# Layer A's first product group: the sums of squares and their factors taken one block later, two squares and a few constants traced later

## Chip, cores, metric

The kernel runs on one core of one Trainium2 chip. The metric is the time of one execution on the device in microseconds (us), as the median of several runs; lower is better. Of each kernel one execution is also recorded by the profiler.

## What is computed

A trunk of two layers on one sequence of 2048 tokens of 1024 values, in float32. The change is in the first projection of the first layer (A). Cut to what matters there:

```python
def rmsnorm(x, g):
    y = x * lax.rsqrt(jnp.mean(x * x, axis=-1, keepdims=True) + EPS)
    return y * g

# layer A
u = rmsnorm(h, norm_a_g[i])
proj = u @ w_in_a[i]                    # q, k, v, forget logits, gate
q, k, v, f_logit, gate = split(proj)
q = rmsnorm(q.reshape(b, s, 16, 64), qnorm_a_g[i])
k = rmsnorm(k.reshape(b, s, 16, 64), knorm_a_g[i])
...
o = fox_attention(q, k, v, log_f)       # causal, with a forget bias
h = h + (o * silu(gate)) @ w_out_a[i]
# shared k, v; layer B: sliding-window attention, gate, projection
```

## The kernel before, in words

**Products.** The 2048 tokens are 16 blocks of 128 (`tb`). A product in float32 is made of three products of rounded parts: the high part of the tokens with the high and the low part of the weights, and the low part of the tokens with the high part of the weights. One block times 512 columns of weights is 8 steps (`dt`, 128 rows of the weights each) of three matmuls, 24 matmuls at L757, all added up in one PSUM tile `b2`. There are three such tiles, so block n writes where block n-3 was read out. The products of layer A come in groups of columns; the first group (`gi == 0`) is half of the values `v`.

**The norm.** The gain is folded into the weights (`split_weight`, L484 high part on ScalarE, L485 low part on VectorE), and the row factor 1/sqrt(mean of squares) is applied when a block's products are read out. So the products need no factor, but the read-out does. In layer A the tokens come transposed from memory (`turned`). A block of them passes through: the load (L369, by SyncE's queue), the cast to the high part (L383, ScalarE), the low part (L384, VectorE), the square in place (L389, ScalarE), the sum over the 8 pieces (L391, VectorE, into a tile `ro2`, of which there are two), the sum over partitions (`block_sums`, L400, two small products with a column of ones for a pair of blocks, each recorded as two matmuls), and `rstd`, a chain of six small instructions (L357 VectorE, L358 square root on ScalarE, L359 to L363 VectorE), which writes the factors `r` of the pair.

**When.** `factor(tb, dt)` is called ahead of each step of the first group. At an even block's step 0 it issues the squares of that block and the next, at the same block's step `FACTOR_AT` = 7 the sums over partitions and the chain. After a block's 24 matmuls come its read-out: for the first group `v_tile`, L539 on ScalarE and L540 on VectorE into a tile `st`, then its store (L543). The blocks' loads and these tiles share four slots `st`; odd blocks up to the eleventh and the next group's weights (L438) share two slots `wr`. Loads run three blocks ahead (`LOADED_AHEAD`). At block 8 `vectors()` issues 13 small loads of gains on SyncE's queue, at block 11 `angles()` makes the sine and cosine tables, with one `Sin` on ScalarE at L327 that needs another function table than the square root.

**The order.** The framework's scheduler puts the instructions of each engine into a fixed queue when the kernel is built: among those whose inputs it estimates as ready and whose slots are free, the one that stands first in the program. Where `keep_in_program_order` is called (L400, the small loads), an instruction stays behind all that the program gave its engine earlier. On the chip each engine works its queue in order.

**Constants.** `constants()` makes `ident` on GpSimd, and from it on VectorE `fold` (L227, twice L229, L230) and `identb` (L232). Both are first used in the attention of layer A.

Of the kernel before, what the change touches and what calls it, by code (L numbers as in the profile page):

```python
# [17 lines left out]
ALU = mybir.AluOpType  # L18
# [4 lines left out]
P = 128  # L23
S = 2048
D = 1024
NTB = S // P
NDT = D // P
# [31 lines left out]
LOADED_AHEAD = 3  # L59
QK_LAG = 1  # L60

FACTOR_AT = 7
ROW_AT = 2

JOBS_AT = (0, 3, 6, 9)
# [84 lines left out]
class Trunk:  # L150
# [56 lines left out]
    def constants(self):  # L207
        nc, cp, a = self.nc, self.const, self.a

        def select(view, src, pattern, base, cm, fill):  # L210
            nc.gpsimd.affine_select(
                out=view, in_=src, pattern=pattern, compare_op=ALU.is_ge,
                fill=fill, base=base, channel_multiplier=cm,
            )

        def tile_(name, shape, dt=F32):
            return cp.tile(shape, dt, name=name, tag=name)

        self.ones = tile_("ones", [P, P])
        nc.gpsimd.memset(self.ones, 1.0)  # L220
        self.tri = tile_("tri", [P, P])
        select(self.tri, self.ones, [[1, P]], 0, -1, 0.0)
        self.ident = tile_("ident", [P, P])
        select(self.ident, self.tri, [[-1, P]], 0, 1, 0.0)

        self.fold = tile_("fold", [P, 32])
        nc.vector.tensor_tensor(self.fold, self.ident[:, :32], self.ident[:, 32:64], ALU.add)  # L227
        for c in (64, 96):
            nc.vector.tensor_tensor(self.fold, self.fold, self.ident[:, c : c + 32], ALU.add)  # L229
        nc.vector.tensor_single_scalar(self.fold, self.fold, 2.0, ALU.mult)  # L230
        self.identb = tile_("identb", [P, P], BF16)
        nc.vector.tensor_copy(self.identb, self.ident)  # L232

        self.mask_s = tile_("mask_s", [P, 2, P], BF16)
        nc.gpsimd.memset(self.mask_s, 0.0)
        for i in range(2):
            select(self.mask_s[:, i], self.mask_s[:, i], [[1, P]], 0, -1, NEG)

        self.band = tile_("band", [P, 2, P], BF16)
        nc.gpsimd.memset(self.band, 0.0)  # L240
        select(self.band[:, 0, :], self.band[:, 0, :], [[1, P]], -1, -1, NEG)
        select(self.band[:, 1, :], self.band[:, 1, :], [[-1, P]], 0, 1, NEG)

        self.loads = []
        warm = tile_("warm", [P, 1])
        nc.scalar.activation(warm, self.ones[:, :1], AF.Sqrt)

        def vector(name, n, views):
            t = tile_(name, [P, n])
            for rows, src in views:  # L250
                self.loads.append((t[rows], src))
            return t

        def column(name, src, n):
            return vector(name, n, [(slice(0, P), src.rearrange("(t p) -> p t", p=P))])

        def pair_column(name, src):
            col = src.rearrange("(p o) -> p o", o=1)
            return vector(name, 1, [(slice(0, HD), col), (slice(HD, P), col)])

        def row(name, src, n):
            return vector(name, n, [(slice(0, P), src.to_broadcast([P, n]))])

        self.g_a = column("g_a", a["norm_a_g"][0], NDT)
        self.bf = row("bf", a["b_forget"], H)
        self.g_qa = pair_column("g_qa", a["qnorm_a_g"][0])
        self.g_ka = pair_column("g_ka", a["knorm_a_g"][0])
        self.g_b = column("g_b", a["norm_b_g"][0], NDT)
        self.g_kv = column("g_kv", a["kv_norm_g"], NDT)
        self.g_qb = pair_column("g_qb", a["qnorm_b_g"][0])  # L270
        self.g_kb = pair_column("g_kb", a["knorm_b_g"])
        self.sink = row("sink", a["sinks"], H)
        self.gq16 = row("gq16", a["qnorm_b_g"][:, :ROT], ROT)
        self.nsink = tile_("nsink", [P, H])
# [6 lines left out]

    def vectors(self):

        nc = self.nc
        self.load_vectors(self.loads[1:])
        for t in (self.g_qb, self.g_kb):
            for s in range(2):
                nc.vector.memset(t[s * HD : s * HD + ROT, :], 1.0)
        nc.vector.tensor_single_scalar(self.nsink, self.sink, -1.0, ALU.mult)
# [274 lines left out]
    def normer(self, src):  # L564


        nc, turned = self.nc, len(src.shape) == 4
        uh, ul, blocks, small = {}, {}, {}, {}
        factors = self.sb("r", [P, NTB], bufs=1)
        done = [0, 0]  # L570

        def parts(tb):
            ch, t0 = divmod(tb * P, CH)
            if ch not in uh:
                uh[ch] = self.sb("big", [P, NDT, CH], F32R)
                ul[ch] = self.sb("big", [P, NDT, CH], F32R)
            return (u[ch][:, :, t0 : t0 + P] for u in (uh, ul))

        def load(tb):
            blocks[tb] = xt = self.load_block(src, tb)  # L580
            if not turned:
                _, junk = parts(tb)
                if tb % 2 == 0:
                    small[tb] = self.sb("sm", [P, 4, 8], bufs=4)
                ss = small[tb // 2 * 2][:, 0, tb % 2 : tb % 2 + 1]
                nc.scalar.activation(
                    junk, xt.rearrange("p (c t) -> p c t", t=P), AF.Square, accum_out=ss
                )

        def fetch(n, loads=()):  # L590
            while done[0] < min(n, NTB):
                load(done[0])
                done[0] += 1
                for other in loads:
                    other()
                loads = ()

        def upto(n, loads=()):

            while done[1] < min(n, NTB):  # L600
                fetch(done[1] + LOADED_AHEAD, loads)
                loads = ()
                tb = done[1]
                self.split_block(blocks[tb], turned, *parts(tb))
                done[1] += 1

        def factor(tb, dt):

            both = (tb, tb + 1)
            if tb % 2:  # L610
                return
            if turned and dt == 0:
                for b in both:
                    blocks[b] = self.block_squares(blocks[b])
            if dt == FACTOR_AT:
                sm = self.sb("sm", [P, 4, 8], bufs=4) if turned else small[tb]
                ss = self.block_sums([blocks[b] for b in both], tb) if turned else None
                self.rstd(sm, 2, D, ss=ss, out=factors[:, tb : tb + 2])

        return upto, factor, uh, ul, factors, fetch  # L620

    def projections(self, normed, groups, row, later=None, pre=None, hook=None, first=None):
# [75 lines left out]
        for gi, grp in enumerate(groups):  # L698
# [35 lines left out]
                continue  # L734
            q, v = grp.get("qk"), grp.get("v")
            rope = self.rotary(q["rope"]) if q and "rope" in q else None
            late = []
            for tb in range(NTB):
                norm(tb + NORM_AHEAD)
                if gi == 1 and tb == ROW_AT:  # L740
                    self.rstd_row(factors, row)
                r0 = factors[:, tb : tb + 1]
                if gi == 0 and pre is not None and tb in pre:
                    pre[tb]()
                if tb in FORGET_AT and forget:
                    forget.pop(0)()
                if gi and tb in JOBS_AT and jobs:
                    jobs.pop(0)()
                us = slice(tb % 4 * P, (tb % 4 + 1) * P)
                ps = self.ps("b2", [P, CH])  # L750
                for dt in range(NDT):
                    if hook is not None and gi == len(groups) - 1:
                        hook(tb, dt)
                    if gi == 0:
                        factor(tb, dt)
                    for i, (u, k) in enumerate(((uh, 0), (uh, 1), (ul, 0))):
                        nc.tensor.matmul(  # L757
                            ps[:, :n], u[tb // 4][:, dt, us], W[k][dt],
                            start=(dt == 0 and i == 0), stop=(dt == NDT - 1 and i == 2),
                        )  # L760
                if len(late) > QK_LAG:
                    late.pop(0)()
                if q is not None:
                    c0 = q["c0"]
                    qn = self.qk_norm(
# [9 lines left out]
                if v is not None:  # L775
                    self.v_tile(
                        ps[:, v["c0"] : v["c0"] + v["nh"] * HD], v["nh"],
                        v["dst"][v["h0"] : v["h0"] + v["nh"], tb * P : (tb + 1) * P, :].rearrange(
                            "h t e -> t h e"
                        ),  # L780
                        r0,
                    )
            for job in late:
                job()
            if grp.get("forget"):
# [784 lines left out]
```

## Time and profile before

| | us |
|---|---|
| median of 3 runs | 2504.49 |
| lowest and highest run | 2503.91, 2506.16 |
| profiled execution, its own time | 2501.05 |
| its span (first to last instruction) | 2499.3 |

In the span TensorE (PE) is busy 98%, VectorE (DVE) 72%, ScalarE (ACT) 52%, GpSimd (POOL) 37%. The rows that a page or a view gives are read like this: in a row of the timeline stand the start from the span's begin, the duration, the engine, the line of the kernel, the operation, what it writes and reads, the number of instructions merged into the row, and in brackets the idle time of the engine ahead of it with what ended it. SPq is SyncE's queue of DMA issues; PEld is TensorE's loading of the stationary operand, beside its matmuls. Buffer numbers are left out of names, so that `b` is a tile `b2`. The first group of products runs from about 8 to 105 us.

### The profile page before, as it was taken

What the parts mean: (1) busy time and instruction counts of PE and PEld (TensorE: products, weight loads), DVE (VectorE), ACT (ScalarE), POOL (GpSimd) and SP (SyncE); (2) the same over time, 40 slices, a digit from 0 to 9 for tenths busy, and PEclk for the clock granted to TensorE, in tenths of its full rate; (3) what the DMA queues carried; (4) which work ended last, traced back from release to release, by engine and by line L of the source; (5) the groups of instructions that cost most, each with busy time, mean ns of one, the idle gap of its engine ahead of it and who ended that gap; (6) DMA issues with size and microseconds to landing.
All of it is one profiled execution on the core that took longest, in us unless ns stands there. A gap on an engine that the chain in (4) does not pass through costs nothing.

```text
span 2499.3 us, 37273 instructions
## 1 busy us (share of the span) xinstructions
PE 2450.7 (98%) x12256; PEld 2048.9 (82%) x12256; DVE 1798.3 (72%) x4279; ACT 1307.5 (52%) x2553; POOL 920.6 (37%) x611
## 2 busy tenths in 40 slices
PE   8999999999999999999999999999999999899999
PEld 6788899988888887877877778888888888788887
DVE  7656667736888888888888965556666434888885
ACT  5423333414777777777777761145332213677674
POOL 0000000013777777777777752200011001355543
PEclk9999999999999999999999999999999999999999
DMA  5656545687545655565465559965443424665561
GB/s 183 201 160 190 174 147 157 192 273 220 147 144 157 192 147 157 145 198 150 131 193 166 153 168 291 287 214 165 114 127 88 128 97 143 188 170 159 160 170 64
DMA packets 351520, 419.29 MB, mean 168 GB/s; under 512 B 64928, under 2 KB 248256, under 8 KB 345152
## 3 DMA queue, kind: packets, MB, share of 16 engines
q1 hardware_dynamic: 351328, 416.92, 57.3%
q8 instruction: 97, 1.59, 0.3%
q14 instruction: 95, 0.78, 0.1%
HBM read 265.29 MB, written 151.40 MB: 167 GB/s over the span
## 4 chain that ended last, share of the span: by engine, by line
PE 48%; DVE 4%; DMA 2%; ACT 2%; issue 1%; POOL 1%; SPq 0%; POOLq 0%; ACTq 0%; DVEq 0%
PE b L757 9%; PE pb L1404 6%; PE b L1220 5%; PE pa L1025 4%; PE pb L1059 3%; PE pb L720 3%; PE b L720 3%; PE b L347 2%; PE mx L934 2%; PE sc L983 2%; PE pa L1337 2%; PE sc L982 2%; DMA wr<-wg 1%; PE b L1282 1%; PE b L1279 1%
## 5 line engine op out<-in xcount | busy, mean ns | idle before, releaser
L757 PE MATMUL b<-wh,big 128*128 128x512 f32 (+3 forms) x2560 | 769.9, 375 | 8.9 <-ACT wh L484 8.9
L1001 POOL TENSOR_TENSOR big<-st,big 128x1024 fp32r<-128x1024 f32 (+1 forms) x320 | 659.7, 2076 | 273.6 <-ACT big L1000 171.8
L757 PEld LDWEIGHTS b<-wh,big 128*128 128x128 f32 x2560 | 471.4, 188 | 79.3 <-ACT wh L484 10.9
L757 PE MATMUL b<-wl,big 128*128 128x512 f32 (+3 forms) x1280 | 473.7, 370 | 1.7 <-DVE wl L485 1.7
L1010 DVE TENSOR_TENSOR ac<-ac,st 128x512 f32<-128x512 f32 (+3 forms) x576 | 355.0, 616 | 53.2 <-ACT st L997 24.5
L997 ACT ACTIVATE st<-sc 128x512 f32<-128x512 f32 (+1 forms) x512 | 274.9, 584 | 157.6 <-PE sc L983 79.4
L1025 PE MATMUL pa<-big 128*128 128x512 f32 (+3 forms) x1280 | 327.1, 370 | 3.1 <-POOL big L1001 1.0
L1000 ACT CAST big<-st 128x1024 fp32r<-128x1024 f32 (+1 forms) x320 | 295.5, 924 | 8.0
L757 PEld LDWEIGHTS b<-wl,big 128*128 128x128 f32 x1280 | 241.4, 189 | 38.3 <-DVE wl L485 5.8
L1025 PEld LDWEIGHTS pa<-big 128*128 128x128 f32 x1280 | 222.8, 190 | 49.1 <-ACT sq L1033 16.8
L945 DVE CUSTOM_DVE_ANT_0 mx<-mx,rot 128x128 f32<-128x128 f32 (+3 forms) x240 | 210.5, 877 | 39.6 <-PE mx L934 34.5
L493 ACT ACTIVATE sq<-b,r 128x512 f32<-128x512 f32 (+2 forms) x128 | 77.8, 608 | 301.2 <-PE b L757 298.1
L982 PE MATMUL sc<-big 128*128 128x512 f32 (+3 forms) x640 | 231.1, 365 | 1.3 <-DVE st L540 1.1
L983 PE MATMUL sc<-big 67*128 67x512 f32 (+3 forms) x640 | 229.7, 368 | 0.0
L934 PE MATMUL mx<-big 66*128 66x128 f32 (+3 forms) x660 | 192.1, 365 | 10.4 <-DVE mt L945 9.8
L1059 PE MATMUL pb<-wh,wr 128*128 128x512 f32 x488 | 179.4, 399 | 3.7 <-DMA wr<-wg 3.1
L495 DVE TENSOR_REDUCE sm<-sq 128x8 f32<-128x512 f32 (+2 forms) x128 | 74.9, 585 | 138.9 <-ACT sq L493 138.7
L857 POOL MEMSET rot<- 128x1024 bf16 x1 | 1.0, 952 | 421.0 <-PE pb L347 421.0
L934 PEld LDWEIGHTS mx<-big 66*128 66x128 f32 x660 | 113.6, 191 | 50.0 <-DVE mt L945 20.2
L1307 POOL TENSOR_TENSOR st<-st,rs 128x1024 f32<-128x1024 f32 (+1 forms) x64 | 118.0, 1843 | 93.4 <-DVE rs L1306 88.1
L982 PEld LDWEIGHTS sc<-big 128*128 128x128 f32 x640 | 121.7, 190 | 23.2 <-DVE st L540 1.5
L983 PEld LDWEIGHTS sc<-big 67*128 67x128 f32 x640 | 121.7, 190 | 21.2
(258 smaller groups left out, 4349.3 us busy)
## 6 DMA issues: line engine op xcount, KB each, us to landing
wr<-wg SPq DMA_DIRECT2D x62, 512.0 KB
va<-st SPq DMA_DIRECT2D x32, 512.0 KB
ka<-st SPq DMA_DIRECT2D x64, 256.0 KB
ut<-big SPq DMA_DIRECT2D x16, 1024.0 KB
big<-ka SPq DMA_DIRECT2D x16, 1024.0 KB
big<-qa SPq DMA_DIRECT2D x16, 1024.0 KB
qb<-st SPq DMA_DIRECT2D x64, 256.0 KB
big<-qb SPq DMA_DIRECT2D x16, 1024.0 KB
```

What stands on the lines that cost most here:

```text
L720: nc.tensor.matmul(ps, W[k][dt][:, ft * P : (ft + 1) * P], u[ch][:, dt, :], start=(dt == 0 and i == 0), stop=(dt == NDT - 1 and i == 2),)
L757: nc.tensor.matmul(ps[:, :n], u[tb // 4][:, dt, us], W[k][dt], start=(dt == 0 and i == 0), stop=(dt == NDT - 1 and i == 2),)
L934: mm = nc.tensor.matmul(ps[:, b, :wb], qb[:66, i * P : (i + 1) * P], kb[:66, k0 + b * wb : k0 + (b + 1) * wb], start=True, stop=True,)
L945: nc.vector.tensor_tensor_reduce(out=lg, in0=lg, in1=mask, scale=1.0, scalar=NEG, op0=ALU.add, op1=ALU.max, accum_out=f_(o),)
L982: nc.tensor.matmul(o, ka[:, ks], qa[:, qs], start=not (last and n_), stop=False)
L983: nc.tensor.matmul(o, kb[:, ks], qb[:, qs], start=False, stop=not diag)
L997: nc.scalar.activation(pf[:, off : off + w], ps[:, :w], AF.Exp, scale=HD**-0.5)
L1000: nc.scalar.copy(ph[:, :tw], pf[:, :tw])
L1001: nc.gpsimd.tensor_tensor(pl[:, :tw], pf[:, :tw], f_(ph[:, :tw]), ALU.subtract)
L1010: nc.vector.tensor_tensor(a_, a_, pf[:, off : off + w], ALU.add)
L1025: nc.tensor.matmul(pv[:, q0 : q0 + w], v[:, k, :], src[:, off : off + w], start=(p == 0 and n_ == 0 and i == 0), stop=(last and n_ == 1 an ...
L1059: nc.tensor.matmul(ps, w[:, dt // 2 % 2, wk, dt % 2, :], us[dt][uk], start=(dt == 0 and i == 0), stop=(dt == NDT - 1 and i == 2),)
```

## The change

Four edits, all in the first group of layer A or ahead of it. (1) `factor`: the sums over partitions and the chain of a pair are issued at the odd block's step 3 (`TURNED_AT`) in place of the even block's step 7, four steps later. (2) The read-out of an even block, which needs the factor, is held until then: the read-out is now a function `evict`, and for an even block of layer A's first group it is issued at the next block's step 3, behind the chain; an odd block's stays behind its matmuls. (3) The squares of blocks 0 and 1 are issued at block 0's step 6 (`SQUARES_AT`) in place of step 0; those of the other pairs stay at the even block's step 0. (4) `fold` and `identb` are made in `vectors()`, at block 8, behind the issue of its small loads. Layer B's use of these functions keeps its order.

```diff
         self.fold = tile_("fold", [P, 32])
-        nc.vector.tensor_tensor(self.fold, self.ident[:, :32], self.ident[:, 32:64], ALU.add)
-        for c in (64, 96):
-            nc.vector.tensor_tensor(self.fold, self.fold, self.ident[:, c : c + 32], ALU.add)
-        nc.vector.tensor_single_scalar(self.fold, self.fold, 2.0, ALU.mult)
         self.identb = tile_("identb", [P, P], BF16)
-        nc.vector.tensor_copy(self.identb, self.ident)
...
     def vectors(self):
...
         self.load_vectors(self.loads[1:])
+        nc.vector.tensor_tensor(self.fold, self.ident[:, :32], self.ident[:, 32:64], ALU.add)
+        for c in (64, 96):
+            nc.vector.tensor_tensor(self.fold, self.fold, self.ident[:, c : c + 32], ALU.add)
+        nc.vector.tensor_single_scalar(self.fold, self.fold, 2.0, ALU.mult)
+        nc.vector.tensor_copy(self.identb, self.ident)
...
         def factor(tb, dt):
 
-            both = (tb, tb + 1)
-            if tb % 2:
-                return
-            if turned and dt == 0:
-                for b in both:
+            t0 = tb // 2 * 2
+            if turned and (tb, dt) == (t0, 0 if tb else SQUARES_AT):
+                for b in (t0, t0 + 1):
                     blocks[b] = self.block_squares(blocks[b])
-            if dt == FACTOR_AT:
+            if (tb, dt) == ((t0 + 1, TURNED_AT) if turned else (t0, FACTOR_AT)):
                 sm = self.sb("sm", [P, 4, 8], bufs=4) if turned else small[tb]
-                ss = self.block_sums([blocks[b] for b in both], tb) if turned else None
-                self.rstd(sm, 2, D, ss=ss, out=factors[:, tb : tb + 2])
+                ss = self.block_sums([blocks[b] for b in (t0, t0 + 1)], tb) if turned else None
+                self.rstd(sm, 2, D, ss=ss, out=factors[:, t0 : t0 + 2])
...
                     if gi == 0:
                         factor(tb, dt)
+                        if held and dt == TURNED_AT:
+                            held.pop()()
...
                 if len(late) > QK_LAG:
                     late.pop(0)()
+                if gi == 0 and pre is not None and tb % 2 == 0:
+                    held.append(partial(evict, ps, tb))
+                else:
+                    evict(ps, tb)
```

## Rows read from the trace of the kernel before

**Rows 1.** The page: the span, and the busy time, share of the span and instructions of each engine.

```profile
span 2499.3 us, 37273 instructions
...
PE 2450.7 (98%) x12256; PEld 2048.9 (82%) x12256; DVE 1798.3 (72%) x4279; ACT 1307.5 (52%) x2553; POOL 920.6 (37%) x611
```

**Rows 2.** Busy time of the engines in three stretches of the first group (start and end in us, length, then busy us and instructions of PE, PEld, DVE, ACT, POOL, the granted clock of TensorE, the share of the DMA engines, GB/s).

```profile
8.24:17.40 9.16, 8.30 (x27) 5.61 (x28) 9.02 (x16) 7.07 (x10) 0.00 (x0) 1.00 0.65 256
28.50:85.10 56.60, 56.60 (x258) 46.98 (x259) 39.78 (x59) 26.98 (x35) 0.00 (x0) 1.00 0.68 195
85.10:105.20 20.10, 18.56 (x84) 15.06 (x84) 16.74 (x41) 11.28 (x16) 0.00 (x0) 1.00 0.52 138
```

**Rows 3.** The waits of the first 130 us, those of TensorE and of its weight loads among them (who waited for whom, us in total, times, longest).

```profile
PE b L757 <- ACT wh L484: 8.9, 2, 8.2
...
PE pa L400 <- DVE ro L391: 1.8, 3, 0.8
PE b L757 <- DVE wl L485: 1.1, 2, 0.9
...
PEld b L757 <- DVE st L540: 0.4, 1, 0.4
```

**Rows 4.** The timeline of VectorE in the first 17 us: the weights' low parts (L485), block 0's sum of squares (L391) and the first three of the five constants' instructions (L227, L232, L229); the last two (L229, L230) lie ahead of the second and of the third L485 row.

```profile
8.22 1.42 DVE L485 SCALAR_TENSOR_TENSOR wl<-big,g_a,wh 128x512 fp32r<-128x512 f32 x2 [1.57 <-ACT wh L484]
9.78 1.98 DVE L391 TENSOR_REDUCE ro<-st 128x128 f32<-128x1024 f32 x1
11.67 0.18 DVE L227 TENSOR_TENSOR fold<-ident 128x32 f32<-128x32 f32 x1
11.77 0.22 DVE L232 CAST identb<-ident 128x128 bf16<-128x128 f32 x1
11.91 0.18 DVE L229 TENSOR_TENSOR fold<-fold,ident 128x32 f32<-128x32 f32 x1
12.01 0.74 DVE L485 SCALAR_TENSOR_TENSOR wl<-big,g_a,wh 128x512 fp32r<-128x512 f32 x1
...
12.77 0.75 DVE L485 SCALAR_TENSOR_TENSOR wl<-big,g_a,wh 128x512 fp32r<-128x512 f32 x1
...
13.52 2.73 DVE L485 SCALAR_TENSOR_TENSOR wl<-big,g_a,wh 128x512 fp32r<-128x512 f32 x4
```

**Rows 5.** The timeline of TensorE: its first matmul, and the sums over partitions (L400) of the pairs (2,3), (4,5), (6,7), (12,13) and (14,15), the last two in two parts, with the first matmul behind the sums of (4,5), and the pair of matmuls with which block 14 ends and block 15 begins.

```profile
8.24 0.79 PE L757 MATMUL b<-wh,big 128*128 128x512 f32 x1 [8.24 <-ACT wh L484]
...
28.22 0.50 PE L400 MATMUL pa<-ones,ro 128*128 128x1 f32 x4
...
39.61 0.50 PE L400 MATMUL pa<-ones,ro 128*128 128x1 f32 x4
39.97 0.49 PE L757 MATMUL b<-wh,big 128*128 128x512 f32 x1
...
50.99 0.50 PE L400 MATMUL pa<-ones,ro 128*128 128x1 f32 x4
...
85.16 0.28 PE L400 MATMUL pa<-ones,ro 128*128 128x1 f32 x2
86.20 0.38 PE L400 MATMUL pa<-ones,ro 128*128 128x1 f32 x2 [0.77 <-DVE ro L391]
...
97.45 0.28 PE L400 MATMUL pa<-ones,ro 128*128 128x1 f32 x2
98.50 0.38 PE L400 MATMUL pa<-ones,ro 128*128 128x1 f32 x2 [0.77 <-DVE ro L391]
...
99.29 0.83 PE L757 MATMUL b<-wh,big 128*128 128x512 f32 x2
```

**Rows 6.** The timeline of VectorE from 79 to 100 us: sums of squares of blocks 12 and 13 (L391), the first and the last step of the chain of the pair (10,11) (L357, L363), and the read-outs of blocks 10 and 11 and of 12 and 13 (L540).

```profile
79.83 2.02 DVE L391 TENSOR_REDUCE ro<-st 128x128 f32<-128x1024 f32 x1 [1.13 <-ACT st L389]
81.77 0.15 DVE L357 TENSOR_SCALAR sm<-pa 128x2 f32<-128x2 f32 x1
...
83.55 0.16 DVE L363 SCALAR_TENSOR_TENSOR r<-sm 128x2 f32<-128x2 f32 x1
84.18 1.97 DVE L391 TENSOR_REDUCE ro<-st 128x128 f32<-128x1024 f32 x1 [0.47 <-ACT st L389]
86.06 1.39 DVE L540 SCALAR_TENSOR_TENSOR st<-b,r,st 128x512 fp32r<-128x512 f32 x2
...
98.81 1.41 DVE L540 SCALAR_TENSOR_TENSOR st<-b,r,st 128x512 fp32r<-128x512 f32 x2 [0.37 <-ACT st L539]
```

**Rows 7.** The timeline of ScalarE: a weight of the second group (L484, at block 11's products), and from 94 us the square roots of the pairs (12,13) and (14,15) (L358), the table loads, `Sin` (L327) and the read-outs of blocks 12 and 13 (L539).

```profile
69.39 0.71 ACT L484 ACTIVATE wh<-wr,g_a 128x512 fp32r<-128x512 f32 x1
...
94.02 0.20 ACT L358 ACTIVATE sm<-sm 128x2 f32<-128x2 f32 x1
...
96.49 1.28 ACT L327 ACT_TABLE_LOAD   x1
97.78 0.42 ACT L327 ACTIVATE cossin<-cossin 128x256 f32<-128x256 f32 x1
98.11 1.25 ACT L539 ACTIVATE st<-b,r 128x512 fp32r<-128x512 f32 x2
99.37 1.28 ACT L358 ACT_TABLE_LOAD   x1
100.67 0.20 ACT L358 ACTIVATE sm<-sm 128x2 f32<-128x2 f32 x1
```

More of the change, by code (lines that the diff above doesn't have):

```diff
@@ L62 @@
 FACTOR_AT = 7
+TURNED_AT = 3
+SQUARES_AT = 6
 ROW_AT = 2
@@ L736, in projections, with evict @@
             rope = self.rotary(q["rope"]) if q and "rope" in q else None
[L737 to L741, printed above, removed]
-                r0 = factors[:, tb : tb + 1]
[L743 to L762, printed above, removed]
+            late, held = [], []
+            def evict(ps, tb):
+                nonlocal z
+                r0 = factors[:, tb : tb + 1]
                 if q is not None:
@@ L782, in projections @@
                     )
+            for tb in range(NTB):
+                norm(tb + NORM_AHEAD)
+                if gi == 1 and tb == ROW_AT:
+                    self.rstd_row(factors, row)
+                if gi == 0 and pre is not None and tb in pre:
+                    pre[tb]()
+                if tb in FORGET_AT and forget:
+                    forget.pop(0)()
+                if gi and tb in JOBS_AT and jobs:
+                    jobs.pop(0)()
+                us = slice(tb % 4 * P, (tb % 4 + 1) * P)
+                ps = self.ps("b2", [P, CH])
+                for dt in range(NDT):
+                    if hook is not None and gi == len(groups) - 1:
+                        hook(tb, dt)
+                    if gi == 0:
+                        factor(tb, dt)
+                        if held and dt == TURNED_AT:
+                            held.pop()()
+                    for i, (u, k) in enumerate(((uh, 0), (uh, 1), (ul, 0))):
+                        nc.tensor.matmul(
+                            ps[:, :n], u[tb // 4][:, dt, us], W[k][dt],
+                            start=(dt == 0 and i == 0), stop=(dt == NDT - 1 and i == 2),
+                        )
+                if len(late) > QK_LAG:
+                    late.pop(0)()
+                if gi == 0 and pre is not None and tb % 2 == 0:
+                    held.append(partial(evict, ps, tb))
+                else:
+                    evict(ps, tb)
             for job in late:
```

## The prediction

> **What bounds the kernel now.** First the page: TensorE is busy 2450.7 of a span of 2499.3 us [rows 1], so whatever this change gives must come out of the 48.6 us in which it is not, and only out of the part of them that lies in the first group. Then the stretches of that group: from 28.5 to 85.1 us TensorE is busy 56.60 of 56.60; it has gaps only from 8.24 to 17.4 (8.30 of 9.16, with pauses inside long matmuls besides) and from 85.1 to 105.2 (18.56 of 20.10) [rows 2]. Then the waits: 8.2 us for the first weight, which nothing here touches, 0.9 for a low part of a weight, 1.8 in three waits for sums of squares (L400 behind L391), 0.4 for a PSUM tile not yet read out [rows 3].
>
> How much is lost in all follows from a rate. Behind the sums of (4,5) 48 matmuls run from 39.97 to 50.99, 0.230 us each, and the four small products take 0.36 (39.61 to 39.97): 11.38 a pair of blocks [rows 5]. From the first matmul at 8.24 to the sums of (2,3) at 28.22 lie 69 matmuls and four small products, 15.9 + 0.36 = 16.2 us; the trace takes 20.0, so 3.8 are lost at the start. From the sums of (12,13) to those of (14,15), 85.16 to 97.45, it is 12.29 in place of 11.38: 0.9 lost, since the second part waits until L391 of block 13 is done (84.18 + 1.97 = 86.15) [rows 5, 6]. The wait at 98.50 is of the same size, 0.9. Block 15's beginning took 0.83 for two matmuls, 0.2 more than the 0.63 of such a pair where none waits: block 12's read-out held its PSUM tile until about 98.81 + 0.7 = 99.5 [rows 5, 6]. Together 3.8 + 0.9 + 0.9 + 0.2 = 5.8 us. That is the ceiling of the change in this group, 0.23% of the span.
>
> **Constants (edit 4).** The five instructions stand between block 0's sum and the third low part: 11.67 to 12.01, 0.34 us; the next two low parts start 0.76 and 0.75 apart, where undisturbed ones are 2.73 / 4 = 0.68 apart: 0.15 more [rows 4]. So 0.5 us on VectorE, which has no idle time there, in front of low parts that TensorE waits for. At block 8 the same five cost at most the same 0.5 if they come in front of something awaited, and nothing in one of VectorE's gaps (39.8 busy of 56.6 [rows 2]). They issue no DMA; the 13 loads ahead of them are SyncE's and stay. I take -0.5, bounds -0.5 and +0.5.
>
> **First squares (edit 3).** The sum over block 0 takes 9.78 to 11.67, 1.9 us, ahead of the third low part [rows 4]. Yet in the program all weights already stand ahead of the squares, at step 0 as at step 6; the squares came first because the third weight wasn't thought ready. Nor does the scheduler keep near TensorE: a weight of the second group was made at 69.39, at block 11 [rows 7]. Only matmuls lie between steps 0 and 6, so I expect the order on ScalarE and VectorE to stay, and this edit to do nothing: 0, taken from these two rows. The other bound: if the squares do fall back, the low parts come 1.9 earlier and the squares' 1.9 is still owed before the first factors, -1.9 to +1.9.
>
> **Sums four steps later (edit 1).** Four steps are 12 matmuls, 2.75 us. The sums of (12,13) would be asked for at 85.16 + 2.75 = 87.9, behind 86.15: the two waits of 0.9 go, and the 0.3 that is left of the 1.8 for the first pair [rows 3] probably with them. Instructions and small products stay the same in number. What is queued behind: L400 is pinned in TensorE's queue, so a sum that is still late there stops all matmuls, as now. And there are two tiles `ro2`: the next pair's L391 can't write before L400 has read, 2.75 later than now. For block 12 (L391 at 79.83, the pair before read about 11.38 ahead of 85.16, at 73.8) there are 6 us of cover [rows 5, 6]; without it the blocks' slots and loads would be late by the difference.
>
> **Held read-outs (edit 2).** This is where the gain can be lost. Block n+3 needs block n's tile. Now the sums are read 17 steps ahead of that, afterwards 13, so the way from the sums to the end of the even block's read-out has 2.75 us less. Yet today it isn't the sums that set the read-out: the chain of (10,11), whose sums were there at about 73.8, began only at 81.77, behind block 12's L391 (which waited for its load's way through ScalarE), and its read-out at 86.06, behind block 13's L391 [rows 6]. Block 10's tile is free at 86.8 and block 13 begins at about 86.20 + 0.3 + three matmuls = 87.2: 0.4 us to spare; block 12's was 0.2 late. So a TensorE that is earlier by more than 0.4 at block 13, or by anything at block 15, waits for the read-out of VectorE and ScalarE, whose pace is set by the blocks' loads, slots and the stores of even blocks, which now stand later in SyncE's queue too. The loads themselves get earlier only by what VectorE gains at the start, 0.5.
>
> **The sum.** Block 15's start is set by block 12's read-out, 0.5 earlier by the constants; behind it stand the 24 matmuls and now also the small products of (14,15), +0.36, which were in block 14. At the change of groups 0.9 us of waits for the second group's weights remain (8.9 - 8.2 and 1.1 - 0.9 [rows 3]); the square root of (14,15) with its table load, 99.37 to 100.87 [rows 7], now comes behind some of those weights; I take -0.3 of the 0.9, bounds 0 and -0.9. In all -0.5 + 0.36 - 0.3 = -0.4 us, with bounds of about -1.5 and +1.2. The profiled execution took 2501.05 (1.75 around its span), the median of the runs 2504.49, 3.4 above; the difference is put on the median: 2504.1, own range 2503.0 to 2505.7.
>
> **Rivals.** *The read-outs come along* (if the scheduler puts the even read-outs ahead of the next block's squares, since they now stand together): both waits, the first pair's rest, the 0.2 at block 15, the constants and 0.3 at the change of groups, -1.8 - 0.3 - 0.2 - 0.5 - 0.3 = -3.1, 2501.4; if the first squares fall back too, -5.0, 2499.5. For it: 5.8 us of loss are there. Against it: 0.4 us to spare at block 13.
>
> *The chain slips by one sum of squares* (slower): the chain of (10,11) began 2.4 ahead of block 13's L391 (81.77, 84.18); with the sums 2.75 later it can fall behind it. Then L357 starts at 86.15, the factor comes 1.9 later (81.77 to 83.71), 88.1, read-out of block 10 by L539 and L540 some 1.4 (98.11 to 98.81, and 0.7) later, 89.5 against the 87.2 at which block 13 began: +2.3, with +0.36 - 0.3 it is +2.4, 2506.9 [rows 6, 7]. It decides from the 0.4 to spare on; if (12,13) slips as well, another 2.3, 2509.2.
>
> *Sin goes ahead of the root.* The root of (12,13) ran at 94.02, 2.5 ahead of the table load for `Sin` at 96.49 [rows 7]. If the later chain puts it behind, it waits for `Sin` (98.20) and a load of 1.3: 99.5, then some 1.9 for chain and 1.4 for the read-out less what overlaps, 102 to 102.8 against 99.5: about +2.6, with the other terms 2507.2. Loads here cost what their rows show, 96.49 to 97.78 and 99.37 to 100.67, 1.3 from load to next function. The Trainium skill (ScalarE: Activation LUTs, What ACT_TABLE_LOAD costs) puts a switch at 2.66 us, half of it a drain; by that estimate this rival would give 2508.6. The trace agrees with its 1.283 for the load and shows no drain behind it, so I leave it at 1.3.
>
> **How the numbers follow.** Forecast 0.48; read-outs come along 0.26, half of it with the squares moved; the chain slips 0.18, a quarter of it twice; Sin first 0.08. A measurement of this kernel can tell about 0.2%, 5.0 us, from no change. Faster by that: most of the 0.13 at 2499.5 lies on the edge, 0.09 with some reordering farther on. Slower by that: the double slip and reordering, 0.06. Same 0.85. The range takes in 2499.5 and the single slip and Sin first by its rows: 2499.0 to 2508.5, leaving about 0.07 at either end.
>
> **What the changed profile would show.** Low parts 0.68 apart from the third on, none of L227 to L232 there; block 0's L391 still between the second and the third low part (else edit 3 works, and the first low parts are 1.9 earlier). No wait of L400 at pairs (12,13) and (14,15). The wait of L757 for L540 at blocks 13 or 15 grown from 0.4 to about 2 us: that carries the forecast; if it is gone, the first rival holds; if L357 of (10,11) stands behind block 13's L391, the second; if L358 of (12,13) stands behind `Sin`, the third. The prediction is wrong if the first group's end moves by more than 2 us, or if anything behind the second group moves by itself.

## The result and the profile after

The changed kernel takes 2507.82 us, the median of 22 runs, beside 2502.3 for the kernel before: a ratio of 1.0018 with a 95% interval of 1.0011 to 1.0024, some 4.5 us more (2.8 to 6.0). The means of these runs are 4.4 us apart, the medians 5.5. The forecast was 0.4 us less. The ratio of the kernel with the constants alone, below, leaves out one run of 3418.81 us, in which the granted clock was 0.655. The profiled execution took 2507.14. Its page, span and busy times [rows 1]:

```profile
span 2505.1 us, 37266 instructions
...
PE 2452.8 (98%) x12256; PEld 2050.0 (82%) x12256; DVE 1798.7 (72%) x4279; ACT 1308.0 (52%) x2553; POOL 920.1 (37%) x611
```

The work is the same. Two of the stretches of [rows 2], with the same columns:

```profile
28.50:85.10 56.60, 54.49 (x249) 44.68 (x248) 39.08 (x55) 25.69 (x34) 0.00 (x0) 1.00 0.66 195
85.10:105.20 20.10, 18.31 (x85) 14.95 (x84) 14.56 (x39) 11.47 (x16) 0.00 (x0) 1.00 0.42 131
```

The stretch in which TensorE had no gap now has gaps of 2.1 us (56.60 - 54.49), and the one that was to lose its gaps still has 1.8 (20.10 - 18.31). Who waited, in the waits of the first 130 us, TensorE's alone [rows 3]:

```profile
PE b L786 <- ACT wh L489: 9.1, 2, 8.7
PE b L786 <- DVE st L545: 3.8, 2, 2.0
PE b L786 <- DVE wl L490: 0.8, 2, 0.5
```

The waits for sums of squares, 1.8 us before, are gone. In their place stand two for a read-out, 3.8 us: matmuls (L786, before L757) that can't begin because the PSUM tile they write isn't read out yet (L545, before L540). The timeline of TensorE has them at the beginnings of blocks 3 and 13 [rows 5 for before, where neither waits]:

```profile
31.06 0.47 PE L786 MATMUL b<-wh,big 128*128 128x512 f32 x1 [1.99 <-DVE st L545]
...
90.42 0.47 PE L786 MATMUL b<-wh,big 128*128 128x512 f32 x1 [1.79 <-DVE st L545]
```

**Block 3** needs block 0's tile, and that needs the factors of blocks 0 and 1. The chain that makes them has five small instructions on VectorE (L362, L364, L365, L366, L368; L357 to L363 before) and a square root on ScalarE behind the first. VectorE's timeline of it, first before, then after:

```profile
21.59 0.16 DVE L357 TENSOR_SCALAR sm<-pa 128x2 f32<-128x2 f32 x1
21.66 2.01 DVE L391 TENSOR_REDUCE ro<-st 128x128 f32<-128x1024 f32 x1
23.59 0.15 DVE L359 RECIPROCAL sm<-sm 128x2 f32<-128x2 f32 x1
23.66 1.99 DVE L391 TENSOR_REDUCE ro<-wr 128x128 f32<-128x1024 f32 x1
25.57 0.15 DVE L360 TENSOR_TENSOR sm<-sm 128x2 f32<-128x2 f32 x1
25.75 0.16 DVE L361 SCALAR_TENSOR_TENSOR sm<-sm 128x2 f32<-128x2 f32 x1
25.94 0.16 DVE L363 SCALAR_TENSOR_TENSOR r<-sm 128x2 f32<-128x2 f32 x1
26.92 1.41 DVE L540 SCALAR_TENSOR_TENSOR st<-b,r,st 128x512 fp32r<-128x512 f32 x2 [0.82 <-ACT st L539]
```

```profile
21.86 0.14 DVE L362 TENSOR_SCALAR sm<-pa 128x2 f32<-128x2 f32 x1
21.93 2.00 DVE L396 TENSOR_REDUCE ro<-st 128x128 f32<-128x1024 f32 x1
23.86 0.15 DVE L364 RECIPROCAL sm<-sm 128x2 f32<-128x2 f32 x1
23.93 1.20 DVE L389 TENSOR_TENSOR big<-st,big 128x1024 fp32r<-128x1024 f32 x1
25.05 0.14 DVE L365 TENSOR_TENSOR sm<-sm 128x2 f32<-128x2 f32 x1
25.12 2.00 DVE L396 TENSOR_REDUCE ro<-wr 128x128 f32<-128x1024 f32 x1
27.05 0.14 DVE L366 SCALAR_TENSOR_TENSOR sm<-sm 128x2 f32<-128x2 f32 x1
27.12 1.21 DVE L389 TENSOR_TENSOR big<-wr,big 128x1024 fp32r<-128x1024 f32 x1
28.26 0.14 DVE L368 SCALAR_TENSOR_TENSOR r<-sm 128x2 f32<-128x2 f32 x1
...
30.17 1.41 DVE L545 SCALAR_TENSOR_TENSOR st<-b,r,st 128x512 fp32r<-128x512 f32 x2 [1.68 <-ACT st L544]
```

Both chains begin at nearly the same time. In the queue of before two large instructions lie between their links, in that of after four, one in every gap: 21.59 to 26.10 becomes 21.86 to 28.40. The two more are low parts (L389), of block 4 in `st` and of block 5 in `wr`, which in before stand behind the read-out. The read-out then loses another 1.0 us to a square on ScalarE, whose timeline of after is:

```profile
28.36 1.06 ACT L394 ACTIVATE wr<-wr 128x1024 f32<-128x1024 f32 x1 [2.08 <-DVE big L389]
29.45 1.27 ACT L544 ACTIVATE st<-b,r 128x512 fp32r<-128x512 f32 x2
```

For block 4 SyncE's queue shows where its early low part comes from; before, then after:

```profile
5.19 20.86 SPq L369 DMA_DIRECT2D wr<-in_x_t  x3
26.11 0.42 SPq L369 DMA_DIRECT2D st<-in_x_t  x1
```

```profile
5.29 0.61 SPq L374 DMA_DIRECT2D wr<-in_x_t  x1
5.95 0.44 SPq L374 DMA_DIRECT2D st<-in_x_t  x1
20.83 6.65 SPq L374 DMA_DIRECT2D wr<-in_x_t  x2
```

The load of block 4 into a slot `st` was issued at 26.11 and is now issued at 5.95. A read-out also takes one of the four slots `st`; the even block's, held, stands later in the program, and the scheduler gave the slot to the load. Block 5's load is as early in both, and why its low part moved up too no row says.

**Block 13** needs block 10's tile. The chain of (10,11) [rows 6 for before: 81.77 to 83.71, ahead of block 13's sum of squares] in VectorE's timeline of after:

```profile
80.49 1.23 DVE L389 TENSOR_TENSOR big<-st,big 128x1024 fp32r<-128x1024 f32 x1 [3.00 <-ACT big L388]
81.63 2.00 DVE L396 TENSOR_REDUCE ro<-st 128x128 f32<-128x1024 f32 x1
83.55 0.15 DVE L362 TENSOR_SCALAR sm<-pa 128x2 f32<-128x2 f32 x1
83.62 2.00 DVE L396 TENSOR_REDUCE ro<-st 128x128 f32<-128x1024 f32 x1
...
86.42 0.15 DVE L365 TENSOR_TENSOR sm<-sm 128x2 f32<-128x2 f32 x1
86.49 1.22 DVE L389 TENSOR_TENSOR big<-st,big 128x1024 fp32r<-128x1024 f32 x1
...
88.03 0.15 DVE L368 SCALAR_TENSOR_TENSOR r<-sm 128x2 f32<-128x2 f32 x1
...
89.52 0.75 DVE L545 SCALAR_TENSOR_TENSOR st<-b,r,st 128x512 fp32r<-128x512 f32 x1
```

Block 13's sum of squares (83.62) has slipped in behind the chain's first link, a low part and small rotary instructions behind later ones: factor at 88.2 in place of 83.7, tile free at 90.3 in place of 86.8. Of these 4.5 us of the factor 1.8 are a later beginning (83.55 after 81.77). It was not the sums that held it: they were there at 79.6 (L405, 79.14 and 0.50). Ahead of the chain in VectorE's queue stand block 13's low part (80.49), for which VectorE was idle for 3.0 us, and block 12's sum of squares (81.63); before, that low part stood behind the first link. The other 2.7 are the gaps between the links: 1.9 us from the first link to the factor before, 4.6 after.

### The profile page after: what moved, and what is told of

It reads as the page before. It is cut to its first block, busy times and chain, and to the rows that moved or that the text cites. A ratio compares the mean times of both kernels' runs of the same rounds, so it can differ in the third digit from the quotient of the medians.

```text
span 2505.1 us, 37266 instructions
## 1 busy us (share of the span) xinstructions
PE 2452.8 (98%) x12256; PEld 2050.0 (82%) x12256; DVE 1798.7 (72%) x4279; ACT 1308.0 (52%) x2553; POOL 920.1 (37%) x611
## 4 chain that ended last, share of the span: by engine, by line
PE 48%; DVE 4%; DMA 2%; ACT 2%; issue 2%; POOL 1%; SPq 0%; ACTq 0%; POOLq 0%; DVEq 0%
PE b L786 9%; PE pb L1417 6%; PE b L1233 5%; PE pa L1038 4%; PE pb L1072 3%; PE pb L723 3%; PE b L723 3%; PE b L352 2%; PE mx L947 2%; PE pa L1350 2%; PE sc L996 2%; PE sc L995 2%; PE b L1295 1%; PE b L1292 1%; PE pa L1233 1%
## 5 line engine op out<-in xcount | busy, mean ns | idle before, releaser
L786 PE MATMUL b<-wh,big 128*128 128x512 f32 (+3 forms) x2560 | 770.7, 375 | 13.2 <-ACT wh L489 9.1
L786 PEld LDWEIGHTS b<-wh,big 128*128 128x128 f32 x2560 | 471.2, 188 | 84.7 <-ACT wh L489 11.1
L786 PE MATMUL b<-wl,big 128*128 128x512 f32 (+3 forms) x1280 | 473.4, 370 | 1.3 <-DVE wl L490 1.3
L786 PEld LDWEIGHTS b<-wl,big 128*128 128x128 f32 x1280 | 241.5, 189 | 37.2 <-DVE wl L490 4.8
L1038 PEld LDWEIGHTS pa<-big 128*128 128x128 f32 x1280 | 223.1, 190 | 49.2 <-ACT sq L1046 16.9
```

The costliest lines, as they stand in the source:

```text
L786: nc.tensor.matmul(ps[:, :n], u[tb // 4][:, dt, us], W[k][dt], start=(dt == 0 and i == 0), stop=(dt == NDT - 1 and i == 2),)
L1038: nc.tensor.matmul(pv[:, q0 : q0 + w], v[:, k, :], src[:, off : off + w], start=(p == 0 and n_ == 0 and i == 0), stop=(last and n_ == 1 an ...
```

## The experiments

The order of instructions on the engines differs between the two kernels in about the first 120 us alone. So beside the total I use a mark (the expectations call it the yardstick): the time from the first matmul to the first transposing matmul of the row factors (L347, after L352) in the second group's block 2. Before it is 8.24 to 117.90, 109.66 us; after, 8.67 to 120.01, 111.34. The mark depends on when TensorE comes to its full pace, which differs between executions of one program (last section). The table gives that time, by the trace's first record of the granted clock; marks are best compared where it is alike. My theory: the sums, four steps later, make the even read-outs late, and the tiles' waits take back more than the sums' waits gave. Rivals: holding the read-out does it whatever the sums do; the squares or the constants do it; something behind the first group does.

| kernel | ratio to before, 95% | mark, us | full pace from, us | tile waits, us (at block) |
|---|---|---|---|---|
| before, two executions | 1 | 109.66, 110.71 | 12.6, 18.0 | none on TensorE |
| after, four executions* | 1.0018 (1.0011 to 1.0024) | 111.34, 112.60, 112.97, 112.47 | 12.5, 12.8, 12.6, 17.4 | 3.5 to 4.1 (3, 13; in the second and the fourth 0.3 of it at 11) |
| constants alone | 1.0000 (0.9991 to 1.0009) | 110.62 | 17.5 | none |
| all but the constants | 1.0021 (1.0012 to 1.0030) | 114.96 | 17.3 | 3.3 (3, 11, 13) |
| held alone, sums as before | 1.0007 (0.9998 to 1.0016) | 110.14 | 17.5 | 1.7 (3) |
| sums at step 0 | 1.0005 (0.9996 to 1.0014) | 109.54 | 15.8 | 1.0 (3) |
| after, fourth tile, two executions | 0.9989 (0.9980 to 0.9998) | 108.47, 108.00 | 16.9, 16.0 | none |
| before, fourth tile | 1.0003 (0.9995 to 1.0011) | 109.31 | 16.0 | none |
| after, shorter chain | 0.9996 (0.9987 to 1.0004) | 108.33 | 17.3 | none |

*Two of the four are of the kernel with `SQUARES_AT` = 0, whose queues have the same order.

**The constants alone.** The kernel before with the constants' lines in `vectors()`:

```diff
-        nc.vector.tensor_tensor(self.fold, self.ident[:, :32], self.ident[:, 32:64], ALU.add)
...
     def vectors(self):
...
+        nc.vector.tensor_tensor(self.fold, self.ident[:, :32], self.ident[:, 32:64], ALU.add)
...
```

> The kernel before with the constants' edit alone. Yardstick for all runs here: the time from TensorE's first matmul to the transposing of the row factors at block 2 of the second group, 109.66 us in the profile of before (8.24 to 117.90) and 111.34 in that of the changed kernel (8.67 to 120.01). Theory (the changed kernel loses at PSUM tiles read out too late, at blocks 3 and 13, because the later sums let large instructions slip between the steps of the factor chain): the constants have no part in it, 109.2 to 109.8, no wait over 0.5 us for a read-out, total time within 0.1% of before. Rival (the constants at block 8 do the harm): 110.5 or more, with a wait at block 11 or 13.

The mark came out at 110.62, outside what was expected, though TensorE's wait for the low part did fall, from 0.85 to 0.52. TensorE's own start hid it: its matmuls ran at half their pace until 17.5 in place of 12.6 us (last section). Beside the execution of before with as late a start, 110.71, the mark is 0.1 less. The total is unchanged.

**All but the constants.** The changed kernel with these lines put back:

```diff
+        nc.vector.tensor_tensor(self.fold, self.ident[:, :32], self.ident[:, 32:64], ALU.add)
...
     def vectors(self):
...
-        nc.vector.tensor_tensor(self.fold, self.ident[:, :32], self.ident[:, 32:64], ALU.add)
```

> The changed kernel with the constants made at the start, as before; all else changed. Theory: both waits for read-outs stay at about 2 us each and the yardstick is 111.2 to 112.0; total 0.1 to 0.25% over before. Rival (constants): the waits go and the yardstick is 109.7 or less.

It is as slow as the whole change and has its waits, 1.20 at block 3, 0.22 at 11, 1.91 at 13. The mark, 114.96, missed the 111.2 to 112.0 expected: TensorE started late here, and behind block 13's wait the granted clock was 0.57 from 92 to 95 us (see below). The loss lies in edits 1 to 3.

**Held alone.** The changed kernel with the sums at the even block's step 7 again; the read-out stays held:

```diff
-            if (tb, dt) == ((t0 + 1, TURNED_AT) if turned else (t0, FACTOR_AT)):
+            if (tb, dt) == (t0, FACTOR_AT):
```

> Sums and factor chain at the even block's step 7, as before, but the read-out of even blocks held to the odd block's step 3, as in the changed kernel (first squares at step 6 and constants at block 8 too). Theory (the lateness of the sums is what costs): the factors are ready as early as before, waits for read-outs under 1 us together, yardstick 109.3 to 110.3; the two waits of 0.8 us for block 13's and block 15's squares are back. Rival (the holding costs): waits of about 2 us at blocks 3 and 13 stay, yardstick 111 or more.

TensorE's wait at block 3 in this kernel:

```profile
32.82 0.50 PE L786 MATMUL b<-wh,big 128*128 128x512 f32 x1 [1.73 <-DVE st L545]
```

It stays although the sums are early, and block 4's load is issued at 6.19, as in after. There my theory fell: at block 3 it is the holding. The wait at block 13 is gone: that one is the sums' being late.

A second expectation failed: the waits for the sums of (12,13) and (14,15) did not come back, though the sums stand at step 7 again. Block 13's sum of squares is done at 84.0 in this kernel (81.99 and 1.97), 86.15 in before; block 12's tokens are there earlier too (cast at 71.41, before 76.40). So holding the read-outs takes these waits away without the four steps.

**Sums at the odd block's step 0.** One step later than before, three earlier than in after:

```diff
-TURNED_AT = 3
+TURNED_AT = 0
```

> The changed kernel with the sums, the chain and the held read-out at the odd block's step 0 in place of step 3: the sums one step later than before in place of four. Theory (each step of delay, 0.69 us, is a step less for the read-out): waits for read-outs shrink by up to 2.1 us each, that is to 0 to 0.5, yardstick 109 to 110. Rival (the place of the sums does not matter, only that they stand in the odd block, with the next block's work in front): waits as in the changed kernel, 111 or more.

No wait at block 13, 0.99 at block 3 (more than the 0.5 expected), and no wait for sums. The same split from the other side.

**First squares back.** The changed kernel with the squares of blocks 0 and 1 at step 0:

```diff
-SQUARES_AT = 6
+SQUARES_AT = 0
```

> The changed kernel with the first squares traced at step 0 again; its instruction order on every engine is that of the changed kernel, so this is a second look at the same program. Theory: 0.1 to 0.25% over before as the changed kernel; waits for read-outs at blocks 3 and 13 of 1 to 2 us each again (less at block 3 if TensorE starts at its lower rate for longer in this execution); what differs from the first profile is what executions differ by. Rival (place of the first squares matters after all): the waits go and the time is that of before.

Every engine has the order of the changed kernel; edit 3 does nothing. The ratio is 1.0017 (1.0008 to 1.0026). So its profile is a second one of the changed kernel, and it shows something that the first does not. Windows of core 0 around block 13's beginning, columns as in [rows 2], and TensorE behind its wait:

```profile
90.00:92.00 2.00, 1.36 (x5) 1.12 (x6) 1.49 (x4) 1.94 (x4) 0.00 (x0) 0.83 0.29 85
92.00:95.00 3.00, 3.00 (x11) 2.51 (x10) 1.33 (x3) 1.71 (x2) 0.00 (x0) 0.54 0.93 282
```

```profile
90.64 0.47 PE L786 MATMUL b<-wh,big 128*128 128x512 f32 x1 [1.89 <-DVE st L545]
...
94.72 0.49 PE L786 MATMUL b<-wh,big 128*128 128x512 f32 x1
```

After the wait of 1.89 the granted clock is 0.54, mostly the lower level of 1.2 GHz. From that wait's end to the first matmul behind the sums it takes 4.08 us, in the first profile of after 90.42 to 92.94, 2.52, for the same matmuls. This wait cost 1.9 + 1.6.

**A fourth tile.** If the tiles' waits are the loss, a fourth tile must turn the change into a gain, with the chain as late as it is. Every fourth block of the group writes a tile `pb`, which lies free there; in the changed kernel, and in the kernel before:

```diff
-                ps = self.ps("b2", [P, CH])
+                ps = self.ps("pb" if gi == 0 and pre is not None and tb % 4 == 3 else "b2", [P, CH])
```

> The changed kernel with a fourth PSUM tile for the first group: every fourth block's products go to the tile pb, unused in that group, so that block n needs the read-out of block n-4. Theory (the loss is the wait for read-outs): no wait of a matmul for a read-out over 0.3 us, the waits for late sums stay away too; yardstick (first matmul to the row factors' transposing) 107.5 to 109 against 111.34; total within 0.1% of before, or below it by up to 0.1%. Rival (the blocks' slots, loads or the sums are late themselves): the waits turn up as others, yardstick 110.5 or more.

> The kernel before with the same fourth PSUM tile. Theory: before loses only 0.2 us for tiles, so yardstick 109.2 to 109.8, total within 0.1% of before. Rival (tiles bound before more than its profile shows): yardstick under 109.

TensorE's waits of the first 130 us, changed kernel with the fourth tile:

```profile
PE b L786 <- ACT wh L489: 9.5, 2, 8.6
PE b L786 <- DVE wl L490: 0.8, 2, 0.5
```

The chain of (0,1) is as long as in after, 22.44 to 29.00, but nobody waits for it. The chain of (10,11) is not as late: with the tile the scheduler's queue changed too, and its factor is there at 82.6 (82.45 and 0.16), 88.2 in after. So at block 3 the run shows the late chain without its price, at block 13 only that the wait is gone. 2501.12 us, a ratio of 0.9989 (0.9980 to 0.9998), faster than both kernels; the kernel before gains nothing from the tile by itself.

**A shorter chain.** The changed kernel without the refining step in layer A's first group: the factor is the reciprocal of the square root as it comes. The chain loses its last three VectorE links, and the factor is less exact.

```diff
+        short = ss is not None and out is not None
...
+        if short:
+            nc.vector.reciprocal(out, t)
+            return out
```

> The changed kernel with the factor chain of layer A's first group cut short: the factor is the reciprocal of the square root, and the refining step of three small VectorE instructions behind it is left out there. Theory (read-outs are late because between two small steps of the chain, each not ready when the one ahead ends, VectorE's queue holds a large instruction of 1.2 to 2 us): from L362 to the factor it takes under 3 us in place of 6.5 for blocks 0 and 1, their read-out is done before 27 us in place of 30.9, no wait at block 3, less than 1 us at block 13; yardstick 108 to 109.5. Rival (read-outs wait for ScalarE or for tokens, not for links of the chain): waits as in the changed kernel.

VectorE's chain of (0,1):

```profile
22.31 0.16 DVE L363 TENSOR_SCALAR sm<-pa 128x2 f32<-128x2 f32 x1 [0.98 <-PE pa L409]
22.39 2.01 DVE L400 TENSOR_REDUCE ro<-st 128x128 f32<-128x1024 f32 x1
24.31 0.17 DVE L366 RECIPROCAL r<-sm 128x2 f32<-128x2 f32 x1
```

22.31 to 24.48, 2.2 us in place of 6.5. The three links left out are 0.5 us of instructions (25.57 to 26.10 in before); the rest of the 4.3 is what lay between them in after. No tile is waited for. Block 4's load is as early as in after (5.84), so the early load alone is not the harm.

**Four more executions**, to tell the kernels' marks from their spread: the changed kernel unchanged, the same with `SQUARES_AT` = 0, the kernel before, and the changed one with the fourth tile.

> The changed kernel, one more profiled look. In the two looks so far block 13 waited 1.8 and 1.9 us for its tile, and in the second TensorE's granted clock fell to half at 91 us, right behind that wait, which cost some 1.7 us more. Theory (a stop of that length is now and then followed by a stretch at the lower clock): the wait is there again, and in at least one of this look and the next the clock is below 1 between 90 and 95 us. Rival (such stretches come at any time): it is 1 there in both.

> The same program as the changed kernel (first squares traced at step 0, same order of instructions), another look; the same expectation as the look before.

> The kernel before, a second profiled look. Theory: no read-out waited for over 0.5 us, granted clock 1 from 24 to 120 us, and the time from the first matmul to the row factors' transposing is 109.7, or up to 2 us more if TensorE starts at the lower rate for longer. Rival: the clock falls in the first group here too.

> The changed kernel with the fourth PSUM tile, a second look. Theory: no read-out waited for, granted clock 1 from 24 to 120 us, yardstick 107 to 108.6, the difference being how long TensorE starts at the lower rate. Rival: yardstick over 109.7.

Marks 112.97, 112.47, 110.71 and 108.00; times 2503.94, 2505.36, 2505.32 and 2500.16. The tiles' waits came again in both of the changed kernel and in neither of the others. Behind block 13's wait the granted clock fell again in the first (0.59 from 92 to 95 us), not in the second.

## Why the prediction was wrong

**Constants: right, two thirds of the size on TensorE.** The five instructions went behind the low parts, which stand 0.68 apart. TensorE's wait for the low part fell by 0.33 (0.85 to 0.52, and 0.5 against 0.9 in every kernel with and without the edit), not by 0.5. The total of the constants alone shows nothing of it (1.0000).

**First squares: right.** Block 0's sum of squares stays between the second and the third low part, and the kernel without the edit has the same queues.

**Sums four steps later: the number came, the reason is not shown.** No wait for sums is left, -1.8 us. But the kernel that holds the read-outs and leaves the sums at step 7 has none either, so the four steps need not be what took them away.

**Held read-outs: here it failed,** at "0.4 us to spare" and at "The loads themselves get earlier only by what VectorE gains at the start, 0.5". The forecast let a TensorE that is earlier run into a read-out that keeps its time, for about 2 us in all. The read-out did not keep its time. That the sums do not set it was right as far as it went (they were there at 79.6, the chain began at 83.55); what was taken as fixed, and moved, is the place of the chain's links in VectorE's queue. At block 13 the second rival's number came: factor at 88.1 forecast, 88.2 measured; tile free at 89.5, measured 90.3; TensorE stopped for 1.79. That was luck: the rival put the whole chain behind block 13's sum of squares (beginning at 86.15, 1.9 us long), but the first link still ran ahead of it (83.55), and the others fell behind other instructions one by one (4.6 us). Sums at step 0 take this wait away, and so do sums at step 7 with the read-outs held, so the four steps are its cause. That rival had 0.18 and the forecast 0.48.

Block 3 was not considered at all. Block 4's load came 20.2 us earlier (26.11 to 5.95), not 0.5. Block 0's tile was free at 27.7 before (26.92 + 0.75, the first of its two rows merged) and at 30.9 after (30.17 + 0.75); the wait is another 1.99. Its cause is the holding, shown by the kernel with early sums that has it too (1.73). That the holding works by the slot, block 4's early load and the fuller gaps is read from the traces and not tried by itself.

The listed waits alone give -1.8 - 0.3 for the low part - 0.3 for the second group's high parts (0.7 to 0.4, as forecast) + 3.8 - 0.2 for block 15's tile = +1.2, where the mark of the first profile says +1.7. The rest shows when a stop is read from one matmul's start to the next, less the 0.23 that is usual: 2.14 us at block 3 (28.69 to 31.06), 1.95 at block 13 (88.24 to 90.42), and 0.28 at block 11, whose stop is too short for the list; 4.4 in place of 3.8. Read so, the whole is -0.3 for the low part, -2.0 for the sums, -0.1 for block 15, -0.2 at the second group and +4.4 = +1.8. Executions with a like start differ by 1.7 to 3.3 in the mark (before 109.66; after 111.34, 112.60, 112.97) and by 1.8 (110.71; 112.47); the half clock behind block 13's wait is in the second and the third of after.

**Sin goes ahead of the root: it did, and cost nothing.** In ScalarE's timeline `Sin` and its table load (L332) now come before the root of (12,13) (L363):

```profile
89.98 1.28 ACT L332 ACT_TABLE_LOAD   x1
91.29 0.42 ACT L332 ACTIVATE cossin<-cossin 128x256 f32<-128x256 f32 x1
...
95.02 1.28 ACT L363 ACT_TABLE_LOAD   x1
96.31 0.20 ACT L363 ACTIVATE sm<-sm 128x2 f32<-128x2 f32 x1
```

TensorE was itself late by then, and block 15 does not wait. The load to the next function took 1.3 us again (95.02 to 96.31), as forecast; the drain that the Trainium skill adds (ScalarE: Activation LUTs, What ACT_TABLE_LOAD costs) shows in neither switch.

**What stays open.** The total says +4.5 (2.8 to 6.0), the marks 1.7 to 3.3. Behind the mark the queues are the same, and no difference shows: from there to the end it is 2381.4 and 2384.5 us in before, 2385.1, 2384.2, 2380.3 and 2382.5 in the changed kernel, means 2382.9 and 2383.0. Two parts of the rest are in the lists of runs. In all 22 runs of the changed kernel 2.02 to 2.13 us of the time lie outside the span, in 35 runs of before 1.72 to 1.84: 0.3 us, for which I know no cause. And the mean granted clock of the 22 runs is 0.9970, that of the 35 is 0.9976; over 2503 us that is 1.5 us, by my estimate, about what the half clock behind block 13's wait would make if it came in nearly every run. Where the clock fell in runs without a profile is not known. With the 1.7 of the first profile this comes to 3.5, inside the interval. That the tile waits are the main cause does not hang on it: where they are gone the same change is at 0.9989 and, with the chain short, at 0.9996.

## What to carry to other kernels

A chain of small dependent instructions on a shared engine costs what the scheduler puts into its gaps, not the sum of its links: the same chain took 4.5 us in one queue and 6.5 in the other, and 2.2 with three links of 0.5 us in all left out. Holding a step back also leaves its buffer free for longer; here, as the traces read, a load took it and its work became the filling. Before a wait is moved off the engine that bounds the kernel, check every consumer of what is made later, the first round included; where a buffer's release is the tight one, one more buffer may be worth more than the order.

## What the hardware showed that I had not expected

**The start differs between executions.** TensorE's first matmuls run 0.43 us apart and later ones 0.23. The change comes at 12.5 to 12.8 us in four executions and only at 15.8 to 18.0 in the ten others, of the same program too. By the sums of (2,3) this makes 1.6 us: 19.98 after the first matmul in one execution of before (28.22 - 8.24), 21.60 in the other (29.95 - 8.35). Two timelines of the same queue, before and the constants alone, each from the wait for the low part on:

```profile
12.81 0.50 PE L757 MATMUL b<-wl,big 128*128 128x512 f32 x1 [0.85 <-DVE wl L485]
13.15 0.63 PE L757 MATMUL b<-wh,big 128*128 128x512 f32 x2
```

```profile
12.63 0.79 PE L757 MATMUL b<-wl,big 128*128 128x512 f32 x1 [0.52 <-DVE wl L485]
13.22 1.05 PE L757 MATMUL b<-wh,big 128*128 128x512 f32 x2
```

A pair takes 0.63 us in one and 1.05 in the other, while the clock column of the windows reads 1.00 for before's stretch [rows 2] and for the other's, 8.40 to 17.00. The traces' first clock records say full speed from 12.57 and from 17.52 on; ahead of the first record the column has nothing to go by and reads 1.00. The spacing of 0.43 is that of the matmuls behind block 13's wait, where the column read 0.54. So a part of the 3.8 us that the prediction counted as lost to VectorE at the start was TensorE's own.

**A wait can cost more than its length.** Behind block 13's wait the granted clock fell in three executions (waits of 1.89, 1.93 and, without the constants, 1.91 us) and not in two (1.75 and 1.79); behind block 3's waits, up to 1.99, never. Where it fell it cost 1.6 us more, worked out above from two executions. What decides it these runs don't show.
